# HGRN2 scores below level 16 on 32-key column tiles, and attention threads that begin 146 and 151 dense steps apart

## The chip, the core and the metric

The kernel runs on one core of a Trainium2 chip. The metric is device time in microseconds. The core has five engines with a queue each: TensorE (PE) for matmuls, VectorE (DVE), ScalarE (ACT), GpSimd (POOL) and SyncE (SP), which issues the DMAs here.

## What is computed

One layer of a hybrid decoder for a prompt of 256 tokens behind 16 meta tokens (one sequence) and for 8 single new tokens: SwiGLU half-step, mixer, SwiGLU half-step, each with a residual and a layer norm. The mixer projects 2048 features to ten blocks of 2048, runs 8 retention heads and 16 HGRN2 heads, gates both and projects back. The change lies in the HGRN2 heads, whose scores carry a decay for each pair of positions and feature:

```python
def hgrn2_chunk(S, q, k, v, logf):
    ...
    b = jnp.cumsum(logf.astype(jnp.float32), axis=2)
    causal = jnp.tril(jnp.ones((C, C), dtype=bool))
    diff = b[:, :, :, None, :] - b[:, :, None, :, :]
    decay = jnp.exp(jnp.where(causal[None, None, :, :, None], diff, -jnp.inf)).astype(q.dtype)
    A = jnp.einsum('bhid,bhjd,bhijd->bhij', q, k, decay)
    o = jnp.einsum('bhij,bhjv->bhiv', A, v) + jnp.einsum('bhid,bhdv->bhiv', q * jnp.exp(b).astype(q.dtype), S)
```

The new tokens take one step of the same recurrences on their own states (8 x 128 x 128 per HGRN2 head, 8 x 256 x 256 per retention head), which are read from and written back to memory.

## The kernel before

**Dense products.** All weights stream through one path: SP loads 512 KB (`raw`, L184, eight 128x128 blocks), ACT rounds it to a high part `whi` (L187), DVE takes the rest `wlo` (L188); each of these pools has three buffers. `dense` (L217) then issues three matmuls for a block, of 280 columns (16 meta, 256 prompt, 8 new tokens) or 264 where the meta tokens aren't needed. The columns are kept in two halves, one at an offset of `XH` = 148 elements (592 bytes) in tiles of `XP` = 296. The kernel is FFN 1 (0 to 758 us), mixer (758 to 1810), w_out and FFN 2 (1810 to 2607).

**The mixer** has eight units, each of one retention head and two HGRN2 heads. For unit u the program projects q, k, v, f (96 steps of dense, a step being one 128-feature slice for two outputs, six matmuls) and the gates of unit u-1 (64 steps). The attention work is written as two Python generators per unit, `mix_hg` and `mix_ret`. Each dense step calls `pump`, which counts down each running thread; a thread whose count is over issues its next piece of work, and the number that it yields is its next wait in steps. `start(generator, wait)` sets the first wait. So PE's order is fixed by these counts, and attention matmuls stand between dense ones. The order of the other engines' instructions is set by a scheduler from the program.

In unit 0, 32 steps are counted, in each later unit 160. HGRN2's thread starts when the value projection `i_h` is out, with a wait of 20 (unit 0), 46 (unit 1) or 3; retention's when `v_r` is out, with 24 (unit 1) or 3. That puts HGRN2's start at steps 20, 126, 243, 403 and on by 160, retention's at 35, 152, 291 and on by 160. A thread must be done before its gates' evacuation (L680 to L700) reads its output. Between pieces lie waits such as `W_LEVEL + 2 * (s <= 2 or u == 1) + calm`, with `calm` 2 in most units.

**Scores of HGRN2.** For level s, pairs of positions are those where the query lies in an odd block of s positions and the key in the even block ahead of it; K and Q are multiplied by products of f (the tiles T) as the level grows. Levels 16, 32 and 64 are matmuls on column tiles (L820, L825). Below that, before the change: the diagonal and levels 1 and 2 are five products q*k of 256 on DVE (`pr`, L239), split in high and low parts (ACT L224, DVE L225), and summed over the features on PE by a matrix of ones (L236, targets `pd` and `pl`); levels 4 and 8 are four fp32 matmuls of 128 keys by 192 columns (L801). Each result is masked into the score tile `acch` by DVE (L789, L883, L805). The high and low products live in the buffers `smh` and `vbh`, which also take the new tokens' states (`load`, L753 to L757).

**The new tokens' states.** DMAs bring the states (`smh`, `smr`), ACT scales them (L905, L1066), DVE adds k times v (L906, L1069), where v comes back from memory broadcast to all partitions (`vbh`, `vbr`); PE reads the result out in 32-column tiles (`pq` L932, `pqr` L1083).

Of the kernel before, what the change touches and what calls it, by code (L numbers as in the profile page):

```python
# [11 lines left out]
F32R = mybir.dt.float32r  # L12
# [6 lines left out]
P = 128  # L19
# [16 lines left out]
XP = 296  # L36
# [11 lines left out]
MASKS = {1: [0], 2: [1, MASKED], 4: [2], 8: [3, MASKED + 1]}  # L48
W_LEVEL = 6

# [77 lines left out]
def trunk(ctx: ExitStack, tc: tile.TileContext, A, O):  # L128
# [417 lines left out]
    with tc.tile_pool(name="yp", bufs=1) as yp:  # L546
# [7 lines left out]
        with tc.tile_pool(name="mp", bufs=1) as mp:  # L554
# [61 lines left out]
            def start(gen, wait):  # L616
                threads.append([gen, wait])

            def project(groups):
                for grp in groups:  # L620
# [4 lines left out]
                    if grp[0] == (QKV_ORDER[0], 0):  # L625
                        outs = norm1.first(block, outs, x0s)
                    elif grp[0] == (QKV_ORDER[2], 0):
                        v = st["i_h"] = tmp("v", (P, 2, T))
# [9 lines left out]
            def evacuate(n, c0, c1, o0, o1, b0, b1):  # L638
# [14 lines left out]
                elif n == "i_h":  # L653
                    v = st.pop("i_h", None)
                    if v is None:
                        v = tmp("v", (P, 2, T))
                        nc.scalar.copy(v[:, 0, :], o0)
                        nc.scalar.copy(v[:, 1, :], o1)

                    start(mix_hg(c0 // 2, st["f"], st["k"], st["q"], v), {0: 20, 2: 46}.get(c0, 3))  # L660
# [11 lines left out]
                elif n == "v_r":  # L672
                    v = tmp("v", (P, 2, T))
# [59 lines left out]
            def mix_hg(u, f, k, q, v):  # L733

                calm = 2 if u != 1 and u < HR - 1 else 0
# [49 lines left out]
                yield 9  # L785
                pd = mx_bank("pd")
                sums(pd, hilo, slice(0, 2))
                for h in range(2):
                    nc.vector.tensor_tensor(  # L789
                        out=acc[:, 2 * P * h : 2 * P * (h + 1)].rearrange("p (b c) -> p b c", b=2),  # L790
                        in0=pd.rearrange("p (b c h) -> p h b c", b=2, h=2)[:, h],
                        in1=ident.unsqueeze(1).to_broadcast([P, 2, P]), op=ALU.mult)
                Tt = f
                for s in LEVELS:
                    if s == 4:


                        for h in range(2):
                            pl = mx_bank("pl")
                            for b in range(2):  # L800
                                nc.tensor.matmul(  # L801
                                    pl[:, 192 * b : 192 * b + 192], K[:, h, NMETA + b * P : NMETA + b * P + P],
                                    Qm.rearrange("p i (x c) -> p i x c", x=4)[:, :, 2 * h + b, :], start=True, stop=True)
                            for i, (sl, mi) in enumerate(((4, MASKS[4][0]), (8, MASKS[8][0]), (8, MASKS[8][1]))):
                                nc.vector.copy_predicated(  # L805
                                    acc[:, 2 * P * h : 2 * P * (h + 1)].rearrange("p (b n t s) -> p b n t s", b=2, t=2, s=sl)[:, :, :, 1, :],
                                    msk[:, mi, :P].rearrange("p (b n s) -> p b n s", b=2, s=sl),
                                    pl[:, :384].rearrange("p (b i n s) -> p b i n s", b=2, i=3, s=sl)[:, :, i])
                    elif s != 8:
                        pl = mx_bank("pl")  # L810
# [4 lines left out]
                    for h in range(2 if s > 8 else 0):  # L815
# [12 lines left out]

                    if s == NMETA:
                        Tt = Tt[:, :, 1:]  # L830
                    k0 = 0 if s < NMETA else NMETA
                    n = LP - k0
                    nb = n // s
                    m = nb // 2
                    t2 = Tt[:, :, :nb].rearrange("p h (n t) -> p h n t", t=2)
                    kv = K[:, :, k0:].rearrange("p h (n t s) -> p h n t s", t=2, s=s)
                    qv = Q.rearrange("p h (n t s) -> p h n t s", t=2, s=s)
                    mq = SEQ // (2 * s)
                    mul(kv[:, :, :, 0, :], kv[:, :, :, 0, :], t2[:, :, :, 1].unsqueeze(3).to_broadcast([P, 2, m, s]))
                    if s != 4:  # L840
                        mul(qv[:, :, :, 1, :], qv[:, :, :, 1, :], t2[:, :, m - mq :, 0].unsqueeze(3).to_broadcast([P, 2, mq, s]))
                    Tn = tmp(f"T{2 * s}", (P, 2, m))
                    mul(Tn, t2[:, :, :, 0], t2[:, :, :, 1])
                    Tt = Tn
                    if s == 1:

                        q4 = Q.rearrange("p h (n t i) -> p h n t i", t=2, i=2)[:, :, :, 1, :]
                        hilo = [tmp("prod" + t, (P, 2, SEQ), dt=F32R, tag=t, bufs=2) for t in ("smh", "vbh")]
                        for j in range(2):
                            pr = tmp(f"pr{j}", (P, SEQ))  # L850
                            mul(pr.rearrange("p (h n i) -> p h n i", h=2, i=2), q4,
                                K[:, :, NMETA + j :: 4].unsqueeze(3).to_broadcast([P, 2, SEQ // 4, 2]))
                            split(hilo[0][:, j], hilo[1][:, j], pr)
                    if s == 2:

                        Qm = tmp("Qm", (P, 3, 2 * P), tag="smh", bufs=2)
                        qf = Q.rearrange("p h c -> p (h c)")
                        odd = [qf.rearrange("p (n t s) -> p n t s", t=2, s=sl)[:, :, 1, :] for sl in (4, 8)]
                        nc.scalar.copy(Qm[:, 0, :].rearrange("p (n s) -> p n s", s=4), odd[0])
                        t4 = Tt[:, :, NMETA // 4 :].rearrange("p h (n t) -> p h n t", t=2)[:, :, :, 0]  # L860
                        q4 = Q.rearrange("p h (n t s) -> p h n t s", t=2, s=4)[:, :, :, 1, :]
                        mul(q4, q4, t4.unsqueeze(3).to_broadcast([P, 2, 32, 4]))
                        nc.scalar.copy(Qm[:, 1, :].rearrange("p (n s) -> p n s", s=8), odd[1])
                        t4 = Tt[:, :, NMETA // 4 :].rearrange("p h (n t) -> p h n t", t=4)[:, :, :, 1]
                        mul(Qm[:, 2, :].rearrange("p (h n s) -> p h n s", h=2, s=8),
                            Q.rearrange("p h (n t s) -> p h n t s", t=2, s=8)[:, :, :, 1, :],
                            t4.unsqueeze(3).to_broadcast([P, 2, 16, 8]))
                    if s in (4, 8):
                        pass
                    elif s == 64:  # L870
# [4 lines left out]
                    elif s >= 16:  # L875
# [4 lines left out]
                    else:  # L880
                        x = pl.rearrange("p (c j) -> p j c", j=2) if s == 2 else pl.rearrange("p (j c) -> p j c", j=2)
                        for j, mi in enumerate(MASKS[s]):
                            nc.vector.copy_predicated(  # L883
                                acc.rearrange("p (n t s) -> p n t s", t=2, s=s)[:, :, 1, :],
                                msk[:, mi, :].rearrange("p (n s) -> p n s", s=s),
                                x[:, j].rearrange("p (n s) -> p n s", s=s))
                    if s in (16, 32):
                        load(s // 32)
                    if s != 4:
                        yield W_LEVEL + 2 * (s <= 2 or u == 1) + calm  # L890
# [358 lines left out]
```

## Times and profile before

| what | value |
|---|---|
| runs | 2610.65 us median of 3 (2608.11 to 2611.9) |
| profiled execution | 2608.88 us, its span 2607.1 us, granted PE clock 0.999 |
| FFN 1 / mixer / w_out and FFN 2 | 0 to 758 / 758 to 1810 / 1810 to 2607 us |
| a steady unit of the mixer | 130.6 us for 160 dense steps |
| DMA | 206 GB/s on the mean |

How to read it: in a row of waits or of the chain, the first number is the start and the second the duration, in us. In a row of windows come the stretch, its length, and the busy time of PE, PEld (weight load), DVE, ACT and POOL with the number of instructions, then the granted clock, the DMA share and GB/s. In a row of groups: line, engine, operation, output and inputs, shapes and count, then busy us and mean ns of one, then the idle time ahead of them and what ended it. A matmul's recorded duration is longer than the distance to the next, since matmuls are pipelined; what one costs is read from the start of one to the start of the next. An fp32 matmul appears in the trace as two records. Line numbers are those of the kernel before.

### The profile page before, as it was taken

The page shows a single profiled execution, that of the slowest core. Times are in us where ns is not written, and L with a number is a line of the kernel's source. Part 1 is how long each engine was busy: PE and PEld are TensorE (multiplying, and loading weights), DVE is VectorE, ACT ScalarE, POOL GpSimd, SP SyncE. Part 2 cuts the span into 40 slices and gives each one's busy share as a digit, 9 for nine tenths or more (in the row PEclk, how much of TensorE's full clock was granted, in tenths as well). Part 3 has the DMA queues.
Part 4 walks back from the last instruction along what each step waited for, and adds up shares of the span by engine and source line. Part 5 has one row for each costly group of instructions (what it writes and reads, how often), then busy time and mean ns, then how long its engine had stood idle before and what let it go on. Part 6 is the DMA issues. An engine that isn't in the chain of part 4 may idle for free.

```text
span 2607.1 us, 54875 instructions
## 1 busy us (share of the span) xinstructions
PE 2586.9 (99%) x22744; PEld 2554.0 (98%) x22744; DVE 1723.9 (66%) x2907; ACT 1385.2 (53%) x2184; POOL 12.9 (0%) x62
## 2 busy tenths in 40 slices
PE   9999999999999999999999999999999999999999
PEld 9999999999999889999999999999999999999998
DVE  6454444565579787777777777776995555556555
ACT  5444444444456666766666666675564444444444
POOL 0000000000000000000000000000000000000000
PEclk9999999999999999999999999999999999999999
DMA  7555555555556676767676767666556666666664
GB/s 244 183 185 186 186 183 184 185 185 184 183 198 222 219 260 205 262 202 260 206 260 201 262 202 259 207 228 194 193 188 200 195 195 196 196 196 193 199 196 147
DMA packets 154587, 536.17 MB, mean 206 GB/s; under 512 B 17696, under 2 KB 25696, under 8 KB 154336
## 3 DMA queue, kind: packets, MB, share of 16 engines
q1 hardware_dynamic: 154048, 532.37, 63.1%
q8 instruction: 178, 2.92, 0.5%
q14 instruction: 73, 0.60, 0.1%
q10 hardware_dynamic: 288, 0.29, 0.0%
HBM read 501.99 MB, written 30.61 MB: 204 GB/s over the span
## 4 chain that ended last, share of the span: by engine, by line
PE 92%; DVE 4%; DMA 2%; ACT 2%; issue 1%; SPq 0%; POOL 0%; DVEq 0%; POOLq 0%; ACTq 0%
PE up L217 36%; PE dn L217 18%; PE pj_q_r L217 3%; PE wo L217 3%; PE pj_v_r L217 3%; PE pj_i_h L217 3%; PE pj_f L217 3%; PE pj_k_r L217 3%; PE pj_g_r L217 3%; PE pj_q_h L217 3%; PE pj_a_r L217 3%; PE pj_g_h L217 3%; PE pj_a_h L217 3%; DVE wlo L188 1%; DMA out_srp<-sro 1%; PE pqr L1083 1%
## 5 line engine op out<-in xcount | busy, mean ns | idle before, releaser
L188 DVE TENSOR_TENSOR wlo<-raw,whi 128x1024 fp32r<-128x1024 f32 (+1 forms) x869 | 1061.6, 1222 | 735.1 <-ACT whi L187 732.8
L187 ACT CAST whi<-raw 128x1024 fp32r<-128x1024 f32 (+1 forms) x870 | 905.5, 1042 | 906.5 <-PE up L217 415.2
L217 PE MATMUL up<-xh,wlo 128*128 128x280 f32 (+1 forms) x2624 | 725.7, 280 | 0.3 <-DVE wlo L188 0.3
L217 PE MATMUL up<-xh,whi 128*128 128x280 f32 (+1 forms) x2624 | 726.0, 280 | 0.0
L217 PE MATMUL up<-xl,whi 128*128 128x280 f32 (+1 forms) x2624 | 725.4, 279 | 0.0
L217 PEld LDWEIGHTS up<-xh,wlo 128*128 128x128 f32 x2624 | 492.6, 189 | 0.7 <-DVE wlo L188 0.7
L217 PEld LDWEIGHTS up<-xh,whi 128*128 128x128 f32 x2624 | 493.1, 189 | 0.0
L217 PEld LDWEIGHTS up<-xl,whi 128*128 128x128 f32 x2624 | 492.7, 189 | 0.0
L217 PE MATMUL dn<-hh,whi 128*128 128x280 f32 (+1 forms) x1376 | 384.7, 280 | 0.0
L217 PE MATMUL dn<-hl,whi 128*128 128x280 f32 (+1 forms) x1376 | 384.3, 279 | 0.0
L217 PE MATMUL dn<-hh,wlo 128*128 128x280 f32 (+1 forms) x1376 | 384.3, 279 | 0.0
L217 PEld LDWEIGHTS dn<-hh,whi 128*128 128x128 f32 x1376 | 260.1, 189 | 0.1
L217 PEld LDWEIGHTS dn<-hl,whi 128*128 128x128 f32 x1376 | 260.1, 189 | 0.1
L217 PEld LDWEIGHTS dn<-hh,wlo 128*128 128x128 f32 x1376 | 260.1, 189 | 0.0
L217 PE MATMUL pj_g_r<-xh,whi 128*128 128x264 f32 x256 | 76.7, 299 | 0.0
L217 PE MATMUL pj_v_r<-xh,whi 128*128 128x280 f32 x256 | 74.2, 290 | 0.0
L217 PE MATMUL pj_g_h<-xh,whi 128*128 128x264 f32 x256 | 73.5, 287 | 0.0
L217 PE MATMUL pj_v_r<-xh,wlo 128*128 128x280 f32 x256 | 72.4, 283 | 0.3 <-DVE wlo L188 0.3
L217 PE MATMUL pj_k_r<-xh,whi 128*128 128x280 f32 x256 | 72.7, 284 | 0.0
L217 PE MATMUL pj_k_r<-xh,wlo 128*128 128x280 f32 x256 | 72.4, 283 | 0.0
L217 PE MATMUL pj_v_r<-xl,whi 128*128 128x280 f32 x256 | 72.3, 283 | 0.0
L217 PE MATMUL pj_k_r<-xl,whi 128*128 128x280 f32 x256 | 72.3, 283 | 0.0
(403 smaller groups left out, 5283.4 us busy)
## 6 DMA issues: line engine op xcount, KB each, us to landing
raw<-in_w_up SPq DMA_DIRECT2D x343, 512.0 KB, 4.2
raw<-in_w_in SPq DMA_DIRECT2D x320, 512.0 KB, 4.0
raw<-in_w_dn SPq DMA_DIRECT2D x172, 512.0 KB, 3.5
smr<-in_sr SPq DMA_DIRECT2D x32, 512.0 KB, 5.6
out_srs<-smr SPq DMA_DIRECT2D x32, 512.0 KB, 4.8
raw<-in_w_out SPq DMA_DIRECT2D x32, 512.0 KB, 3.6
smh<-in_sg SPq DMA_DIRECT2D x16, 512.0 KB, 4.4
vbr<-vrd SPq DMA_DIRECT2D x16, 512.0 KB, 4.4
```

What stands on the lines that cost most here:

```text
L187: nc.scalar.copy(hi[:, j:jn, :], raw[:, j:jn, :])
L188: nc.vector.tensor_tensor(out=lo[:, j0:j1, :], in0=raw[:, j0:j1, :], in1=hi[:, j0:j1, :].bitcast(F32), op=ALU.subtract)
L217: nc.tensor.matmul(o, w, t, start=start, stop=stop)
L1083: nc.tensor.matmul(pq[32 * j : 32 * j + 32, :256], qdr[:, c, 32 * b : 32 * b + 32], sms[2 * e + c][:, j, :], start=e + c == 0, stop=e + c ...
```

## The change

Four things change.

1. The diagonal and levels 1, 2, 4 and 8 become fp32 matmuls on column tiles of 32 keys: for each tile of 32 keys, 48 columns (three sets of 16 queries, gathered by ACT and DVE in `Qm`), and for the first group 32 columns more, the queries at the keys' own positions, of which the diagonal is taken. The products `pr`, their split and the sums are gone.
2. The threads' first waits are set by formulas, and the waits inside are the same in all units (`CALM` = 2). HGRN2's thread now starts at steps 20, 166, 312, 458, 604, 750, 896 and 1043, retention's at 35, 186, 337, 488, 639, 790, 941 and 1092.
3. The values' tile `v` has two buffers.
4. `XP` is 288, so the halves lie 576 bytes apart.

```diff
-XP = 296
+XP = 288
...
-MASKS = {1: [0], 2: [1, MASKED], 4: [2], 8: [3, MASKED + 1]}
+MASKS = {1: [0], 2: [MASKED, 1], 4: [2], 8: [3, MASKED + 1]}
+CALM = 2
...
-                    start(mix_hg(c0 // 2, st["f"], st["k"], st["q"], v), {0: 20, 2: 46}.get(c0, 3))
+                    start(mix_hg(c0 // 2, st["f"], st["k"], st["q"], v), max(3, 100 - 7 * c0) if c0 else 20)
...
-                    v = tmp("v", (P, 2, T))
+                    v = tmp("v", (P, 2, T), bufs=2)
...
-                    start(mix_ret(c0 // 2, st["q_r"], st["k_r"], v), 24 if c0 == 2 else 3)
+                    start(mix_ret(c0 // 2, st["q_r"], st["k_r"], v), max(3, 67 - 9 * c0 // 2) if c0 else 3)
...
-                hilo = [tmp("prod" + t, (P, 3, SEQ), dt=F32R, tag=t, bufs=2) for t in ("smh", "vbh")]
-                for i in range(3):
-                    pr = tmp(f"pr{i}", (P, SEQ))
-                    if i < 2:
-                        mul(pr, q[:, i, :SEQ], k[:, i, NMETA:LP])
-                    else:
-                        mul(pr.rearrange("p (h c) -> p h c", h=2), Q[:, :, 1::2], K[:, :, NMETA::2])
-                    split(hilo[0][:, i], hilo[1][:, i], pr)
+                def side_by_side(s):
+                    x = tmp("Qm", (P, 3, 2 * P), tag="smh", bufs=2)
+                    part = lambda i, s: x[:, i, :].rearrange("p (h n s) -> p h n s", h=2, s=s)
+                    nc.scalar.copy(part(0, s), odd(s))
+                    scale_q(s)
+                    nc.scalar.copy(part(1, 2 * s), odd(2 * s))
+                    k0 = NMETA // s
+                    t4 = Ts[s][:, :, k0 : k0 + SEQ // s].rearrange("p h (n t) -> p h n t", t=4)[:, :, :, 1]
+                    mul(part(2, 2 * s), odd(2 * s), t4.unsqueeze(3).to_broadcast([P, 2, SEQ // (4 * s), 2 * s]))
+                    return x
+                def blocks(x, s, own=None):
+                    x = x.rearrange("p i (x j c) -> p i x j c", x=4, j=4)
+                    for h in range(2):
+                        pl = mx_bank("pl")
+                        half = pl[:, : 2 * 80].rearrange("p (b c) -> p b c", b=2)
+                        for b in range(2):
+                            for j in range(0, P, 32):
+                                kk = K[:, h, NMETA + b * P + j : NMETA + b * P + j + 32]
+                                o = half[j : j + 32, b, :48].rearrange("p (i c) -> p i c", i=3)
+                                nc.tensor.matmul(o, kk, x[:, :, 2 * h + b, j // 32, :], start=True, stop=True, tile_position=(0, j))
+                                if own is not None:
+                                    nc.tensor.matmul(
+                                        half[j : j + 32, b, 48:], kk, own[:, h, b * P + j : b * P + j + 32],
+                                        start=True, stop=True, tile_position=(0, j))
...
-                yield 9
-                pd = mx_bank("pd")
-                sums(pd, hilo, slice(0, 2))
...
-                                nc.tensor.matmul(
-                                    pl[:, 192 * b : 192 * b + 192], K[:, h, NMETA + b * P : NMETA + b * P + P],
-                                    Qm.rearrange("p i (x c) -> p i x c", x=4)[:, :, 2 * h + b, :], start=True, stop=True)
...
-                    if s == 1:
-                        sums(pl[:, :SEQ], hilo, 2)
-                    elif s == 2:
-                        sums(pl, hilo)
...
+                yield 10 + CALM
+                blocks(Q1, 1, q)
+                scale_q(2)
+                join(2)
+                Q4 = side_by_side(4)
+                scale_k(1)
+                scale_k(2)
+                yield 2 * W_LEVEL - 1 + CALM
+                blocks(Q4, 4)
+                join(4)
...
```

`scale_k(s)`, `scale_q(s)` and `join(s)` are the multiplications of K, Q and T that stood in the loop over the levels before; `odd(s)` is the view of Q's odd blocks. `blocks` also masks its results: one multiplication by the unit matrix of 256 for the diagonal in each head (only with `own`), and three copy_predicated of 128 in each head.

**PE, unit 2, the first scores of HGRN2.** Names: `pd` and `pl` are the score banks, `pj_..` the projections' banks. Before, the four sums stand among the steps of the projection q_r:

```order
L217 MATMUL pj_q_r_12263<-xh_13_9280,wlo_12404 128x264
L236 MATMUL pd<-prodsmh,ones_r 128x512
L236 MATMUL pd<-prodvbh,ones_r 128x512
L236 MATMUL pl<-prodsmh,ones_r 128x256
L236 MATMUL pl<-prodvbh,ones_r 128x256
L217 MATMUL pj_q_r_12262<-xh_14_9284,whi_12403 128x264
```

and in the changed kernel (whose lines 218, 808 and 810 are dense and the two matmuls of `blocks`):

```order
L218 MATMUL pj_a_r_12995<-xh_5_9248,wlo_13028 128x264
L808 MATMUL pl<-Qm,K 32x48
L810 MATMUL pl<-q,K 32x32
L808 MATMUL pl<-Qm,K 32x48
L810 MATMUL pl<-q,K 32x32
L808 MATMUL pl<-Qm,K 32x48
L810 MATMUL pl<-q,K 32x32
```

The pair of rows comes 16 times in one piece, each pair on one column tile and the next pair on the next of four; and the place has moved from q_r of the unit's own projections to the gates of the unit before (`pj_a_r`).

**DVE, unit 3, the updates of both threads between two weight loads.** `wlo` is the low half of a load of weights, `acch` the score tile, `smh` and `ks` the HGRN2 states and retention's scaled keys. Before, one load apart from the next:

```order
L188 TENSOR_TENSOR wlo_14549<-raw_14547,whi_14548 128x8x128
L906 SCALAR_TENSOR_TENSOR smh<-vbh,fk,smh 128x128 x5
L188 TENSOR_TENSOR wlo_14584<-raw_14582,whi_14583 128x8x128
L239 TENSOR_TENSOR K<-K,T_14444 128x2x8x16
L239 TENSOR_TENSOR Q<-Q,T_14444 128x16x16
L906 SCALAR_TENSOR_TENSOR smh<-vbh,fk,smh 128x128 x8
L188 TENSOR_TENSOR wlo_14664<-raw_14662,whi_14663 128x8x128
```

and in the changed kernel:

```order
L189 TENSOR_TENSOR wlo_15175<-raw_15173,whi_15174 128x8x128
L1011 SCALAR_TENSOR_TENSOR ks_8640<-pt,dec,ks_8640 24x128
L255 TENSOR_TENSOR vs_8641<-vt_8636,vs_8641 24x128
L1011 SCALAR_TENSOR_TENSOR ks<-pt,dec,ks 128x128
L240 TENSOR_TENSOR dtab<-psc,dtab 128x400
L973 TENSOR_REDUCE cen<-vt_8636 24x1
L1011 SCALAR_TENSOR_TENSOR ks<-pt,dec,ks 128x128
L974 TENSOR_SCALAR cen<-cen 24x1
L907 SCALAR_TENSOR_TENSOR smh<-vbh,fk,smh 128x128
L240 TENSOR_TENSOR gt<-gs,pj_g_r_14863 128x264
```

The second half of the state update `smh` stood alone between its loads; now it stands with retention's keys, the score table `dtab` and the gates of the unit before.

More of the change, by code (lines that the diff above doesn't have):

```diff
@@ new lines, in blocks @@
+                def blocks(x, s, own=None):
[12 more added lines that the diff above has]
+                                        start=True, stop=True, tile_position=(0, j))
+                        a = acc[:, 2 * P * h : 2 * P * (h + 1)]
+                        if own is not None:
+                            nc.vector.tensor_tensor(
+                                out=a.rearrange("p (b j c) -> p b j c", b=2, j=4),
+                                in0=half[:, :, 48:].unsqueeze(2).to_broadcast([P, 2, 4, 32]),
+                                in1=ident.rearrange("p (j c) -> p j c", j=4).unsqueeze(1).to_broadcast([P, 2, 4, 32]), op=ALU.mult)
+                        for i, (sl, mi) in enumerate(((s, MASKS[s][0]), (2 * s, MASKS[2 * s][0]), (2 * s, MASKS[2 * s][1]))):
+                            n = 16 // sl
+                            nc.vector.copy_predicated(
+                                a.rearrange("p (b j n t s) -> p b j n t s", b=2, j=4, t=2, s=sl)[:, :, :, :, 1, :],
+                                msk[:, mi, :P].rearrange("p (b j n s) -> p b j n s", b=2, j=4, s=sl),
+                                half[:, :, 16 * i : 16 * i + 16].rearrange("p b (n s) -> p b n s", s=sl).unsqueeze(2).to_broadcast([P, 2, 4, n, sl]))
@@ L784, in mix_hg @@
                     yield 1
-                yield 9
-                pd = mx_bank("pd")
-                sums(pd, hilo, slice(0, 2))
[L788 to L793, printed above, removed]
@@ new lines, in mix_hg @@
+                yield 10 + CALM
[8 more added lines that the diff above has]
+                join(4)
+                for s in (4, 8):
+                    scale_k(s)
+                scale_q(8)
+                join(8)
+                yield W_LEVEL + 4 + CALM
+                for s in LEVELS[MASKED:]:
+                    pl = mx_bank("pl")
+                    for h in range(2):
@@ L837, in mix_hg @@
[L837 to L867, printed above, removed]
@@ L868, in mix_hg @@
-                    if s in (4, 8):
-                        pass
-                    elif s == 64:
+                    scale_k(s)
+                    scale_q(s)
+                    join(s)
+                    if s == 64:
                         for b in range(2):
@@ L879, in mix_hg @@
                                 pl[j * s : (j + 1) * s, : 4 * s].rearrange("p (x s) -> p x s", x=4))
[L880 to L886, printed above, removed]
                     if s in (16, 32):
                         load(s // 32)
-                    if s != 4:
-                        yield W_LEVEL + 2 * (s <= 2 or u == 1) + calm
+                    yield W_LEVEL + CALM
+                Tt = Ts[2 * LEVELS[-1]]
                 on = tmp("on_h", (P, 2, TL), bufs=2)
```

62 lines of the change are left out of this document (30 added, 32 removed), and 2 rows, old and new, of the table rows.

## Prediction

> **What bounds the kernel now.** I read the profile's first and fourth parts (busy shares, the chain that ended last), then the windows by stage, the waits of TensorE (PE), the chain again inside single units, and the PE timeline around the instructions that the change replaces.
>
> ```profile
> PE 2586.9 (99%) x22744; PEld 2554.0 (98%) x22744; DVE 1723.9 (66%) x2907; ACT 1385.2 (53%) x2184; POOL 12.9 (0%) x62
> PE 92%; DVE 4%; DMA 2%; ACT 2%; issue 1%; SPq 0%; POOL 0%; DVEq 0%; POOLq 0%; ACTq 0%
> core 0: 2607.1 us, clock 0.999
> 758.00:866.00 108.00, 100.44 (x874) 95.29 (x873) 100.45 (x223) 70.12 (x139) 1.73 (x3) 1.00 0.67 221
> 866.00:972.00 106.00, 102.54 (x937) 97.44 (x936) 84.31 (x183) 69.84 (x145) 1.21 (x3) 1.00 0.67 227
> 1238.60:1368.30 129.70, 129.70 (x1191) 126.94 (x1191) 100.84 (x205) 83.66 (x158) 1.22 (x3) 1.00 0.70 232
> 1498.80:1629.40 130.60, 130.60 (x1191) 127.02 (x1190) 100.95 (x205) 83.61 (x158) 1.22 (x3) 1.00 0.70 231
> 1629.40:1760.00 130.60, 129.21 (x1187) 126.35 (x1186) 103.18 (x213) 87.75 (x164) 2.32 (x14) 1.00 0.66 218
> ```
>
> PE makes up 92% of the chain at a granted clock of 0.999. In a steady unit of the mixer (the third and fourth windows) it is busy in every microsecond, with VectorE (DVE) at about 101 of 130: what PE no longer issues there comes off the end, and DVE work comes off for nothing. Only two units and the last one are otherwise: PE lacks 7.56 us in 758 to 866, 3.46 in 866 to 972 and 1.39 in the last, 12.4 together. A unit is 160 dense steps in 130.6 us, so a step is 0.82 us.
>
> **The change part by part: PE.** What goes is told by the chain inside unit 3, and by the timeline where a burst stands among dense matmuls (columns: start, duration, what).
>
> ```profile
> 1282.49 0.43 PE pd L236 x2
> 1282.92 0.24 PE pl L236 x2
> 1290.23 0.43 PE pl L236 x2
> 1297.81 1.30 PE pl L801 x8
> ...
> 1304.55 0.28 PE L217 MATMUL pj_v_r<-xh,wlo 128*128 128x280 f32 x1
> 1304.76 0.39 PE L825 MATMUL pl<-Q,K 128*16 128x16 f32 x32
> 1305.08 0.39 PE L217 MATMUL pj_v_r<-xh,whi 128*128 128x280 f32 x1
> 1305.30 0.28 PE L217 MATMUL pj_v_r<-xl,whi 128*128 128x280 f32 x1
> 1305.42 0.28 PE L217 MATMUL pj_v_r<-xh,wlo 128*128 128x280 f32 x1
> ...
> 1220.78 0.28 PE L217 MATMUL pj_a_r<-xh,wlo 128*128 128x264 f32 x1
> 1220.98 1.08 PE L932 MATMUL pq<-smh,qdh 128*32 128x128 f32 x32
> 1221.99 0.38 PE L217 MATMUL pj_g_r<-xh,whi 128*128 128x264 f32 x1
> 1222.21 0.28 PE L217 MATMUL pj_g_r<-xl,whi 128*128 128x264 f32 x1
> ...
> L825 PE MATMUL pl<-Q,K 128*16 128x16 f32 x256 | 3.1, 178 | 0.7 <-DVE K L239 0.7
> L932 PE MATMUL pq<-smh,qdh 128*32 128x128 f32 x256 | 8.6, 276 | 0.0
> ```
>
> Removed per unit: 0.43 + 0.24 + 0.43 + 1.30 = 2.40 us. The four L801 matmuls in the code are eight records, so an fp32 matmul is two records, and one of 192 columns takes 1.30 / 8 = 162 ns, 0.85 ns a column.
>
> Added per unit: 16 matmuls of 48 columns and 16 of 32 for level 1 and 2, and 16 of 48 for levels 4 and 8; that is 96 records on four column tiles, in two bursts. Two bursts of before have this form. A dense matmul with 280 columns follows the one ahead by 0.12 us (1305.30 to 1305.42), with 264 by 0.113. From 1304.55 to 1305.30 the burst of 16 columns cost 0.75 - 2 x 0.12 = 0.51 us. Its 32 records start over 0.39 - 0.18 = 0.21 us, so 6.8 ns apart, and the other 0.30 us go to entering and leaving the tiled form. The burst pq cost 1.43 - 2 x 0.113 = 1.20 us; its 32 records start over 1.08 - 0.28 = 0.80 us, 26 ns apart, so each of four tiles starts one every 104 ns: 0.81 ns a column, the speed of L801, with the four tiles at once. Entering and leaving is 1.20 - 8 x 0.108 = 0.33.
>
> So the second burst is 8 rounds of four tiles x 41 ns (48 columns x 0.85) + 0.32 = 0.65 us. The first is 8 x (41 + 27) + 0.32 = 0.87 us. Sum 1.52; with a little for the short records I take 1.55. **PE wins 0.85 us per unit, 6.8 us in eight.** That rests on four tiles running side by side although x and own, four records in all, follow each other on one tile before the next tile has its turn; pq has only the two records of one matmul there. The other end: no overlap in the first burst, 16 x (2 x 41 + 2 x 27) ns = 2.18 us + 0.32, and the unit is 2.50 + 0.65 - 2.40 = 0.75 us worse, 6.0 us in all. Where only the last record of a tile runs beside the next tile's first, it is 16 x (41 + 41 + 27) ns = 1.74 + 0.32, and the unit is 0.31 us worse, 2.5 in all. I take the gain, since pq shows queued records of one tile not holding up the others.
>
> The Trainium skill, page TensorEngine Tiling (Array Packing), section Instruction Overhead, states about 60 cycles for each matmul however few its columns. Taken as 25 ns of the one PE queue per record (an estimate from that page, a cycle put at the 0.42 ns of a dense column), 96 records and two switches would be 3.0 us for 2.40 removed, and PE 5 us slower in eight units; but the 16-column burst has its records 6.8 ns apart, so here the figure could hold at most on one tile (4 x 6.8 = 27 ns), which leaves the sum as it is. The same page's section Key Properties has a change of tiling mode drain the engine; the 0.30 to 0.33 us per burst agree.
>
> **DVE and ACT.**
>
> ```profile
> L239 DVE TENSOR_TENSOR pr<-Q,K 128x256 f32<-128x256 f32 x24 | 9.6, 421 | 0.2
> L225 DVE TENSOR_TENSOR prodvbh<-pr,prodsmh 128x256 fp32r<-128x256 f32 x40 | 15.7, 417 | 0.0
> L883 DVE COPY_PREDICATED acch<-msk,pl 128x256 f32<-128x256 uint8 x24 | 17.6, 733 | 3.6 <-PE pl L236 3.5
> L805 DVE COPY_PREDICATED acch<-msk,pl 128x128 f32<-128x128 uint8 x48 | 11.3, 290 | 0.0
> L224 ACT CAST prodsmh<-pr 128x256 fp32r<-128x256 f32 x40 | 15.3, 405 | 13.3 <-DVE pr L239 13.1
> ```
>
> Per unit DVE loses five products (2.1 us), five low halves (2.1) and three wide copy_predicated (2.2); it gains one more product of 256 (0.4) and six copy_predicated of 128 (1.7): 4.3 us less. ScalarE (ACT) loses five casts (2.0) and gains two copies of a like size (0.8). In steady units this is worth nothing by itself, since PE covers it. The tiles' new stride (576 B for 592) I cost at nothing: a dense matmul takes 0.12 / 280 = 0.43 ns a column at 592 B, the sums of 512 columns 0.215 / 512 = 0.42 at 1024 B, where the halves alternate. Only the 256-column sum shows more, 0.12 / 256 = 0.47; a tenth on every dense matmul would be over 200 us, and no stride seen does that. v in two buffers and the masks' order add no instruction.
>
> **The new starts.** In units 2 to 6 the HGRN2 thread began 51 dense steps into the unit, the retention thread 48 after it, and the pair repeated each 160. Now they repeat each 146 and 151; in unit 2 HGRN2 begins 120 steps in, retention 25 behind, so for units 1 to 4 both threads' DVE work falls on the same loads. In units 0 and 1 it is looser: 40 steps more between the first two HGRN2 threads.
>
> ```profile
> PE pqr L1083 <- DVE smr L1069: 3.0, 3, 1.9
> PE psr L1048 <- DVE ks L1012: 1.6, 2, 1.0
> PE pl L825 <- DVE Q L239: 1.6, 1, 1.6
> PE pt L1006 <- DVE acch L805: 1.5, 1, 1.5
> 923.43 5.46 DMA smh<-in_sg
> ...
> 932.04 1.23 DVE wlo L188
> ...
> 933.95 1.28 DVE acch L805 x6
> ...
> 960.61 6.28 DMA vbr<-vrd
> ...
> 967.46 1.03 PE pqr L1083 x4
> ```
>
> Two waits of unit 1 come straight from HGRN2 work that stood in DVE's queue (pl on Q 1.6, pt on acch 1.5); I take those 3.1 us as gone. Bounds: nothing, and all 12.4. On the other side stands the crowding: between the rows above, unit 1 has its loads of state, its copy_predicated, the low halves of the weights (wlo, on which dense matmuls wait) and the retention update together on DVE, and PE lost 3.46 us for it. Behind a waiting smr on DVE stands the next wlo, and PE waits for that once its three buffers are used. I take 0.4 us in each of units 1 to 5, 2 us, near the nothing of steady units because 30 us of DVE are free in each and its work falls by 4.3; the other end is 3.46 in each, 17.3.
>
> **Sum.** -6.8 - 3.1 + 2.0 = -7.9 us. The profiled execution took 2608.88 us (span 2607.1 and 1.8 around it): 2601.0. The median of the three runs, 2610.65, is 1.77 above it: **2602.8 us**.
>
> **Rivals.**
> - *Crowding decides (slower).* Place: units 1 to 5, where the smh and smr updates, ks and the level copies of both threads now stand between the same wlo. Price: unit 1's 3.46 each, 17.3, less the gain 6.8 and 3.1: +7.4, 2618 us. It decides from 9.9 us of new waits. For: in the changed order of unit 3 the smh and ks updates alternate, as the rows above show. Against: DVE has 30 us free per unit, and dense products keep three loads ahead.
> - *The tiles do not overlap.* +2.5 to +6.0 for PE instead of -6.8, with the waits as in the sum: 2612 to 2616 us. For: four records in a row on one tile, which no row shows. Against: pq. The Trainium skill's 60 cycles per matmul (TensorEngine Tiling (Array Packing), Instruction Overhead), if they fell one after another, would come out here too; I give that 0.02 of this rival's chance.
> - *All waits of units 0, 1 and 7 go.* -6.8 - 12.4: 2591 to 2596 us. Against: DVE is busy 100.45 of 108 us in the first window, with normalization and its first loads, which the change hardly touches.
> - *The change doesn't pay as it says:* the saved time is eaten by waits of equal size elsewhere, since PE then asks for weights sooner; 2608 to 2611. Against: steady units show no wait at all and DMA shares of 0.70.
>
> **How the numbers follow.** Forecast 0.50 (its own range 2599 to 2607, 0.42 of it below 2605.4), all waits gone 0.13, no overlap 0.12, crowding 0.17, nothing 0.08. A measurement of this kernel can tell about 0.2%, 5.2 us. Faster: 0.42 + 0.13 = 0.55. Slower, above 2615.9: all of crowding, and a third of no overlap for the waits that may come on top, 0.21. Same: the rest, 0.24. From 2593 to 2617 leaves out half of the waits-gone case and half of crowding, some 0.15.
>
> **What would show it.** In a steady unit: the level-1 burst as one piece of about 0.55 us and the level-4 one of 0.33, with dense matmuls back at 0.12 behind each, and the unit 0.85 us shorter wherever PE has no wait. If the first burst takes over 1.7 us, the tiles did not overlap. PE rows waiting for wlo, smr or smh in units 2 to 5 would show crowding; a first window with over 104 us of PE busy would show more waits gone. Dense matmuls off 0.12 us apart would prove me wrong on the stride.

## The result and the profile after

The changed kernel takes **2633.84 us** (median of 4 runs, 2632.35 to 2634.92) against 2609.38 us for the kernel before (2607.12 to 2611.9): a ratio of 1.0091, 95% interval 1.008 to 1.0103. It is 24 us slower, where 2602.8 was forecast. In the profiled execution the span went from 2607.1 to 2633.0 us. The page of the changed kernel, busy shares and chain:

```profile
PE 2594.6 (99%) x23400; PEld 2551.5 (97%) x23400; DVE 1703.5 (65%) x2859; ACT 1368.5 (52%) x2154; POOL 13.7 (1%) x62
PE 84%; DMA 6%; DVE 5%; ACT 3%; issue 2%; SPq 0%; POOL 0%; DVEq 0%; ACTq 0%; POOLq 0%
```

PE's share of the chain fell from 92 to 84%; DMA, DVE and ACT gained it. The waits of PE, by line and what it waited for:

```profile
PE pqr L1082 <- DVE smr L1068: 15.9, 12, 4.4
PE pl L872 <- DVE Q L240: 3.8, 1, 3.8
PE psr L1047 <- DVE ks L1011: 3.1, 4, 1.2
PE pl L808 <- DVE ks L1011: 1.4, 1, 1.4
PE ptk L900 <- DVE K L240: 1.3, 1, 1.3
```

Here psr is the product that gives retention's new prompt state, pqr the read-out of the new tokens' states, `ks` retention's scaled keys, and ptk a transpose of HGRN2's keys. Before, pqr waited 3.0 us in all, psr 1.6. These are the waits of PE's matmuls; pqr's loads of weights (PEld) waited longer, and already before. Their rows, before and changed:

```profile
PEld pqr L1083 <- DVE smr L1069: 12.6, 34, 2.4
PEld pqr L1082 <- DVE smr L1068: 31.1, 47, 4.8
```

Two units by window, where before PE was busy throughout (columns as in the prediction's windows):

```profile
1096.40:1232.70 136.30, 132.42 (x1289) 126.84 (x1288) 99.38 (x205) 80.76 (x158) 1.48 (x3) 0.99 0.69 227
1232.70:1375.60 142.90, 136.87 (x1288) 130.05 (x1288) 101.78 (x210) 87.29 (x165) 1.31 (x4) 0.96 0.68 223
```

A steady unit of 129.7 or 130.6 us is now one of 136 or 143. The same DVE work of about 100 us lies in it, and the granted clock is under 1.

A ledger shows where the time went: the distance from each matmul's start to the next one's, summed over the matmuls of one kind (worked out from the traces; us; the third column is the first experiment below).

| kind | before | changed | changed, old starts |
|---|---|---|---|
| scores below level 16 (sums and L801; L808 and L810) | 18.3 | 12.2 | 10.6 |
| pqr | 29.0 | 50.0 | 24.7 |
| psr | 13.4 | 17.3 | 12.7 |
| pvr, sums for retention's normalization | 3.1 | 1.8 | 1.8 |
| dense of the projections | 912.6 | 920.9 | 912.0 |
| FFN 1, up and gate | 958.2 | 959.1 | 960.7 |
| all, to the last matmul | 2600.6 | 2626.5 | 2588.0 |

The new scores are cheaper, 6.1 us with a wait of 1.4 in them; pqr gives back 20.9 and psr 3.9. PE's own waits for pqr grew by 12.9 us, those of its weight loads by 18.5. The bursts themselves, from the timeline of the changed kernel (first the pieces of the level-1 burst's beginning and end, then the level-4 burst):

```profile
1327.82 0.28 PE L218 MATMUL pj_a_r<-xh,wlo 128*128 128x264 f32 x1
1328.02 0.31 PE L808 MATMUL pl<-Qm,K 128*32 128x48 f32 x8
1328.13 0.25 PE L810 MATMUL pl<-q,K 128*32 128x32 f32 x7
...
1328.87 0.38 PE L218 MATMUL pj_g_r<-xh,whi 128*128 128x264 f32 x1
1329.09 0.28 PE L218 MATMUL pj_g_r<-xl,whi 128*128 128x264 f32 x1
...
1337.63 0.28 PE L218 MATMUL pj_a_h<-xh,wlo 128*128 128x264 f32 x1
1337.84 0.55 PE L808 MATMUL pl<-Qm,K 128*32 128x48 f32 x32
1338.32 0.38 PE L218 MATMUL pj_g_h<-xh,whi 128*128 128x264 f32 x1
1338.54 0.28 PE L218 MATMUL pj_g_h<-xl,whi 128*128 128x264 f32 x1
```

The first costs 1329.09 - 1327.82 - 2 x 0.113 = 1.04 us, the second 0.68: 1.72 for 1.55 forecast, and 2.40 removed. The four tiles do run side by side: the whole first burst took 1.04 us, and one record after another it would have been 2.50 by the prediction's own rates.

### The profile page after: what moved, and what is told of

Read it like the earlier page. It is cut to its first block, busy times and chain, and to the rows that moved or that the text cites. A ratio compares the mean times of both kernels' runs of the same rounds, so it can differ in the third digit from the quotient of the medians.

```text
span 2633.0 us, 56076 instructions
## 1 busy us (share of the span) xinstructions
PE 2594.6 (99%) x23400; PEld 2551.5 (97%) x23400; DVE 1703.5 (65%) x2859; ACT 1368.5 (52%) x2154; POOL 13.7 (1%) x62
## 4 chain that ended last, share of the span: by engine, by line
PE 84%; DMA 6%; DVE 5%; ACT 3%; issue 2%; SPq 0%; POOL 0%; DVEq 0%; ACTq 0%; POOLq 0%
PE up L218 34%; PE dn L218 18%; PE pj_i_h L218 3%; PE pj_q_r L218 3%; PE wo L218 3%; PE pj_k_r L218 3%; PE pj_v_r L218 3%; PE pj_q_h L218 3%; PE pj_g_r L218 2%; PE pj_a_r L218 2%; DVE wlo L189 2%; PE pj_g_h L218 2%; DMA vbr<-vrd 2%; PE pj_f L218 2%; PE pj_a_h L218 2%; DMA smh<-in_sg 2%
```

## The experiments

**Starts or scores.** First the two halves of the change apart. The changed kernel with the old starts:

```diff
-  start(mix_hg(...), max(3, 100 - 7 * c0) if c0 else 20)
+  start(mix_hg(...), {0: 20, 2: 46}.get(c0, 3))
-  start(mix_ret(...), max(3, 67 - 9 * c0 // 2) if c0 else 3)
+  start(mix_ret(...), 24 if c0 == 2 else 3)
```

> The changed kernel with the first waits of before (20, 46, 3 for HGRN2; 24 and 3 for retention); the new scores, the waits inside, the two buffers and the stride stay. Theory A (the new starts cost the time: retention's state update has to be done a fixed number of steps after its thread's start, and now its loads and its DVE work cross those of the HGRN2 thread): about 2604 us, 6 below before, since the new scores alone save 6.0 us of PE; PE's waits at the state read-out (pqr on smr) back at 3 to 5 us in all. Rival B (the rewritten scores, with their copies and masks, delay DVE and ACT whatever the starts): 2620 us or more, pqr waits still over 10.

Measured 2597.31 us, ratio 0.9955 (0.994 to 0.9969): faster than before, and 7 us below the 2604 of theory A; pqr's wait is 4.2, as theory A had it. And the other half, the kernel before with the new starts, the even waits, two buffers for v and `XP` = 288:

> The kernel before with the new first waits, the waits inside as changed, v in two buffers and the stride of 576 B (without which the buffers do not fit); the scores stay on DVE products and sums. Theory A: the starts bring about 30 us of waits, so 2636 to 2642 us, with pqr waits of 15 us or more. Rival B: within 5 us of before, 2606 to 2615.

Measured 2632.9 us, 1.009 (1.0075 to 1.0105); its pqr waits are 8.8 us, not the 15 expected, and its scores wait 6.6 us for Q. So the starts cost 23.4 us with the old scores (the even waits and the stride with them) and 36.5 with the new ones, and all else together wins 12. In the old-start kernel a steady unit has no wait of PE, and takes 128.3 to 129.3 us for 129.7 to 130.6 before:

```profile
1232.75:1362.00 129.25, 129.25 (x1274) 126.08 (x1272) 98.52 (x199) 82.20 (x154) 1.22 (x3) 1.00 0.70 234
1362.00:1490.25 128.25, 128.25 (x1274) 125.76 (x1272) 98.61 (x200) 82.38 (x154) 1.22 (x3) 1.00 0.71 236
```

**How retention's update comes late.** In each unit the state update is a chain: product psr, its copy to `sro` and store, the decay factor (which shares `sro`'s buffer), scaling on ACT, update of the first half on DVE, the second load of values (`vbr`, one buffer), update of the second half, then pqr. The program asks for pqr a fixed number of steps after psr, 23.8 us where nothing waits. In the steady units of before, the second half's updates begin 21 to 22 us after psr; in units 1 to 4 of the changed kernel 26 to 29. There was no room for that. PE's read-out in unit 3 before, and the same 29 records in the fastest kernel below:

```profile
1215.35 3.48 PE L1083 MATMUL pqr<-smr,qdr 128*32 128x256 f32 x29
1208.03 1.89 PE L1083 MATMUL pqr<-smr,qdr 128*32 128x256 f32 x29
```

Before, the last record starts 0.29 us behind the end of the last update in seven of eight units (0.34 in the eighth): the read-out already went at the pace of the updates, one each 0.40 us. A later read-out shows that the late update is all that pqr waits for:

```diff
-                yield 15 + 2 * CALM
+                yield 23 + 2 * CALM
```

> The changed kernel with one wait made longer: retention's state read-out comes 8 steps (6.6 us) later, nothing else. Theory A in its form that the chain of the state update (store of the new state, scale, load of the values, update, twice) is only too late for a fixed point in the program: the pqr waits of 15.9 us fall under 4 and the time to 2612 to 2618 us. Rival C (in the crowded stretch DVE or the DMA queues have too much work for the dense products as well): PE waits as long, then for wlo or further on, and the time stays above 2628.

Measured 2612.05 us, 1.0007 (0.9997 to 1.0016). The waits of pqr are gone; other waits (ptk 5.4, Q 3.7, psr 3.7, wlo 7.4) stay or grow. So the first part holds, with a part of the rival's.

**Which resource.** Three kernels took something from the crowded stretch of the changed kernel. First, less to store (a quarter of retention's and an eighth of HGRN2's new states):

```diff
-  nc.sync.dma_start(O["srs"][u, c, :, 4 * e : 4 * e + 4, :], sm)
+  nc.sync.dma_start(O["srs"][u, c, :, 4 * e : 4 * e + 1, :], sm[:, :1, :])
-  nc.sync.dma_start(O["sgs"][2 * u + h], sm)
+  nc.sync.dma_start(O["sgs"][2 * u + h, :, :1, :], sm[:, :1, :])
```

> The changed kernel with the new tokens' states written back only in part (a quarter of retention's, an eighth of HGRN2's), so that some 2.6 of about 8 MB of attention transfers per unit are gone. If the transfers crowd each other when both threads load and store at once: pqr waits under 6 us and the time at or under 2618 us. If the crowding is on DVE: 2626 to 2634.

Measured 2615.82 us, 1.0032 (1.002 to 1.0043); pqr no longer waits. Then seven of eight of HGRN2's updates on DVE left out (`if b == 0:` ahead of L907):

> The changed kernel without seven of eight of HGRN2's state updates on DVE (k times v isn't added there), some 14 instructions and 4 to 5 us of DVE per unit less, all in the stretch where the two threads cross; the transfers stay. If DVE's queue is what makes retention's update late: pqr waits under 6 us, at or under 2618 us. If it is the transfers: 2626 to 2634.

Measured 2635.77 us, 1.0108 (1.0093 to 1.0123), as slow as with them, and pqr still waits 12.2 us. **The amount of DVE work, on which I had put the crowding, isn't it**, as far as HGRN2's updates go. Then the factor in a tile of its own (`tmp("gam", (P, 1))` for `tmp("sro", (P, 1))`):

> The changed kernel with one tile more: the decay factor of retention's state update gets a buffer of its own, where it shared the one of the outgoing state and so was written only after that store had landed. If the chain of transfers in the retention thread (store, factor, scale, load of the values) is what comes too late at the read-out: pqr waits of 15.9 us fall to about 5 and the time from 2634 to 2612 - 2620 us. If the late part is DVE's queue or the second load of the values: 2628 to 2635.

Measured 2621.43 us, 1.0051 (1.0034 to 1.0068): pqr waits 3.3 us; 12 us are won where 14 to 22 were expected.

The store experiment changed something besides bytes: where the second load of values stands in SP's queue (it leaves 0.5 us after the start of the last update of the first half in all eight units). SP at the update of retention head 3, the changed kernel:

```profile
1237.21 0.64 SPq L1071 DMA_DIRECT2D out_srs<-smr  x1
1239.90 0.33 SPq L185 DMA_DIRECT2D raw<-in_w_in  x1
1240.28 0.43 SPq L1071 DMA_DIRECT2D out_srs<-smr  x1
1242.79 0.33 SPq L185 DMA_DIRECT2D raw<-in_w_in  x1
1243.17 0.45 SPq L1036 DMA_DIRECT2D vbr<-vrd  x1
```

and the same place before:

```profile
1203.93 0.34 SPq L1072 DMA_DIRECT2D out_srs<-smr  x1
1205.81 0.33 SPq L184 DMA_DIRECT2D raw<-in_w_in  x1
1206.61 0.34 SPq L1072 DMA_DIRECT2D out_srs<-smr  x1
1207.00 0.42 SPq L1037 DMA_DIRECT2D vbr<-vrd  x1
```

Before, vbr leaves 0.4 us behind the second store. In the changed kernel a weight load stands between them; it waits for its buffer until 1242.79, and vbr, whose own buffer is free from 1238.73, when the last update of the first half ends, waits behind it. From the start of that update to vbr's issue it is 0.9 to 1.2 us in units 1 to 6 of before (4.8 and 2.3 in units 0 and 7), and 6.5, 4.7, 4.8, 4.9, 4.6, 0.9, 0.9, 3.9 us in the changed kernel's eight units. DVE, the updates that follow in the changed kernel (start, duration, idle before):

```profile
1236.67 2.06 DVE L1068 SCALAR_TENSOR_TENSOR smr<-vbr,k_r,smr 128x256 f32<-128x256 f32 x5
1249.07 0.48 DVE L1068 SCALAR_TENSOR_TENSOR smr<-vbr,k_r,smr 128x256 f32<-128x256 f32 x1 [4.32 <-DMA vbr<-vrd]
```

Two kernels put that load elsewhere. On GpSimd's queue (`nc.gpsimd` for e = 1), and ahead of the weight load on SP:

```diff
-   nc.sync.dma_start(vbs[e], vrow[4 * e : 4 * e + 4, :].partition_broadcast(P))
+   with tc.high_priority():
+       nc.sync.dma_start(vbs[e], vrow[4 * e : 4 * e + 4, :].partition_broadcast(P))
```

> The changed kernel with one transfer on another queue: retention's second load of values (vbr, 512 KB) is issued by GpSimd, whose queue is nearly empty, and no longer by SyncE, where in units 0 to 4 and 7 it stood behind a weight load that waits for its buffer and left 3.9 to 6.5 us after it could have (0.9 us in units 5 and 6, and in the steady units of before). Theory Q (the place in SyncE's queue makes the state update late): the load leaves within 1 us, pqr waits fall from 15.9 to under 5 us, 2610 to 2620 us. Rival T (the transfers crowd each other, so the values land when they do whatever the queue): pqr waits over 10, 2627 us or more.

> The changed kernel with the same transfer kept on SyncE but given the weight loads' priority, so that it stands ahead of the weight load in units 0 to 4 and 7. Theory Q: as with GpSimd's queue, 2610 to 2622 us, unless the first load of values, which gets the priority too, holds weights back. Rival T: 2627 or more.

On GpSimd's queue: 2634.77 us, 1.0098 (1.0083 to 1.0113), nothing won: the time is rival T's, the shorter waits of pqr are theory Q's. First on SP: **2613.18 us**, 1.0016 (1.0007 to 1.0025), 20.7 us won, with vbr's issue 0.5 us behind the update's start in all units and pqr's waits at 0.3 us. The place in SP's queue is thus shown as the largest single cause (the edit gives the first load of values the same priority, but that one leaves 0.5 to 4.3 us ahead of psr here and 0.6 to 4.3 in the changed kernel). What is left, 15.9 us above the old starts, shows as waits for DVE: pl for Q 7.4 us, psr 4.2, ptk 3.9. No run tells what makes those late. GpSimd's load did leave early, 0.8 us behind the update's start, and pqr's waits fell to 4.5, but it took longer to land, 7.4 us at the median (5.5 to 9.1) against 4.2 (3.3 to 5.2) for SP's loads of values in the old-start kernel. DVE stood waiting for it longer, as its rows for the changed kernel and this one show, and PE's waits for wlo rose from 4.0 to 11.9 us:

```profile
DVE smr L1068 <- DMA vbr<-vrd: 19.8, 7, 4.3
DVE smr L1068 <- DMA vbr<-vrd: 31.3, 8, 6.3
```

In the old-start kernel the same move shows what then waits:

> The kernel of the old first waits with the new scores (2597.3 us) and the second load of values on GpSimd's queue. There only units 0 and 1 have it 6.5 and 4.9 us late, and only unit 0 waits (4.2 us): Theory Q 2592 to 2596 us, the steady units unchanged. Rival T: 2596 to 2600.

Measured 2614.27 us, 1.002 (1.001 to 1.0029): 17 us lost where 1 to 5 were to be won. DVE in unit 3, and PE's wait for it over the run:

```profile
1213.48 0.48 DVE L1068 SCALAR_TENSOR_TENSOR smr<-vbr,k_r,smr 128x256 f32<-128x256 f32 x1 [4.83 <-DMA vbr<-vrd]
1213.88 1.22 DVE L189 TENSOR_TENSOR wlo<-raw,whi 128x1024 fp32r<-128x1024 f32 x1
```

```profile
PE pj_g_r L218 <- DVE wlo L189: 12.5, 6, 2.7
```

The update waited 4.83 us for its values, and the weights' low half behind it in DVE's queue held up the dense product. The factor's own tile, which won 12 us in the changed kernel, loses time too with the old starts:

> The kernel of the old first waits with the new scores (2597.3 us) and the factor's own buffer. Its one wait at the read-out left is 4.2 us in unit 0, behind the same chain: if the chain's store is part of it, 2592 to 2596 us; if the second load of the values sets it alone, 2596 to 2599.

Measured 2613.03 us, 1.0019 (1.001 to 1.0028), 15.7 us lost. With the factor free early, ACT's scaling of the first half stands 75 to 108 us earlier and its first updates 1 to 4 us behind psr instead of 10 to 12, and PE now waits for wlo in the gates (4.1 us) and at the outputs (2.6). These waits are less than the loss; where the rest goes was not traced. And the two loosened together, in the changed kernel:

> The changed kernel with both links of retention's update loosened: the second load of values ahead of the weight load on SyncE (alone: 2634 to 2613 us), and the factor in a buffer of its own (alone: 2634 to 2621). If each removes waits of its own: 2598 to 2606 us. If both remove the same waits: 2610 to 2616 us, and what is left of the starts' cost lies elsewhere.

Measured 2620.11 us, 1.0049 (1.0032 to 1.0066): slower than the load's place alone, and above both ranges. They take away the same waits of pqr; that the factor's tile brings its own waits with it, as with the old starts, is my reading.

**Distance or spacing.** Retention 42 steps behind HGRN2 in unit 1 and 48 in the others, HGRN2 still every 146:

```diff
-  start(mix_ret(...), max(3, 67 - 9 * c0 // 2) if c0 else 3)
+  start(mix_ret(...), {2: 80}.get(c0, max(3, 100 - 7 * c0)) if c0 else 3)
```

> The changed kernel with retention starting 42 (unit 1) or 48 steps behind HGRN2 in every unit, as in before, while the HGRN2 threads keep their 146 steps. Theory A in its form that the small distance of 20 to 45 steps between the two threads makes them cross: pqr waits under 6 us, 2606 to 2613 us. Rival D (the spacing of 146 itself, by which the threads meet the evacuations of other projections, costs the time): 2625 us or more.

Measured 2618.64 us, 1.004 (1.0025 to 1.0055), between the two theories: 15 of the 36 us come back, pqr still waits 13.0. The opposite, threads every 160 steps and retention 20 behind HGRN2 (HGRN2's waits 52 in unit 1 and 31 from unit 2, retention's old ones):

> The new scores with threads that repeat every 160 steps as in before, but with HGRN2 starting so late in each unit that retention is only 20 steps behind it, as in the changed kernel's unit 1 (distance 15 in unit 0 as always). If the small distance makes the two threads stand in each other's way in the queues: 2612 to 2630 us, with the second load of values late by over 3 us in the steady units. If the spacing that is no multiple of a unit costs the time: 2597 to 2603 us.

Measured 2636.85 us, 1.0109 (1.0094 to 1.0124), slower than the changed kernel, 39.5 us above the old starts. So spacing that repeats with the unit doesn't help when the distance is small. The HGRN2 threads also stand 28 steps later in the unit here, which this run doesn't tell apart from the distance. The waits of PE in this kernel:

```profile
PE pl L808 <- DVE ks L1011: 10.6, 7, 2.0
PE pl L872 <- DVE Q L240: 10.3, 6, 2.2
PE pqr L1082 <- DVE smr L1068: 9.8, 4, 4.5
```

The first is a wait that no kernel with a distance of 48 has: HGRN2's scores `pl` take the bank in which retention's transposed keys lie until DVE's ks have read them (the rows name ks as the releaser; that it is the bank is my reading, since ks and pl share no other tile). vbr is 3.5 to 5.2 us behind the update in all later units here. So the small distance, or the later place that came with it, costs; the uneven spacing costs as well, by the 48-step kernel (21 us above the old starts). It was not tried which positions in a unit are bad, and why the old starts get their good place in SP's queue from unit 2 on stays open: a scheduler sets that order. Where threads repeat every 160 steps it comes out nearly the same in each unit, good (0.9 us with the old starts) or bad (3.5 to 3.6 here).

**A faster version.** The old starts with the read-out later, 8 steps in unit 0 and 2 in the others, and then with vbr ahead of the weight load too:

> The kernel of the old first waits with the new scores, with retention's read-out 8 steps later in unit 0 and 2 steps later in the others. If what is left there is only the read-out asked for too early, the 4.2 us of unit 0 and 0.3 to 0.9 us in each steady unit go: 2589 to 2594 us. If the wait only moves on to the next one that needs the same chain: 2595 to 2599.

> The fastest so far (old first waits, new scores, read-out 8 and 2 steps later: 2592.9 us) with the second load of values ahead of the weight load. Only units 0 and 1 have it late (6.5 and 4.9 us): 2588 to 2592 us. If giving it priority holds weights back: 2594 or more.

Measured 2592.94 us, 0.9936 (0.9921 to 0.9951), and **2590.38 us, 0.9928 (0.9913 to 0.9943)**, the lowest, though the two intervals overlap. In the latter pqr has no wait left, and its ledger row is 14.7 us for 29.0 before: of the 18 us won, 14 stand there, more than the scores gave. All units from the third on now take the same time:

```profile
1228.18:1356.43 128.25, 128.25 (x1274) 125.67 (x1272) 98.68 (x199) 82.62 (x155) 1.22 (x3) 1.00 0.70 235
1356.43:1484.68 128.25, 128.25 (x1273) 125.67 (x1272) 98.82 (x199) 82.76 (x154) 1.22 (x3) 1.00 0.70 236
```

## Why the prediction was wrong, point by point

- **PE's term was right.** -6.8 us forecast; the bursts of 1.72 us make it 0.68 per unit, 5.4 in eight, and the ledger has -6.1 with a wait in it. The rival that the tiles do not overlap is out (it wanted over 1.7 us in the first burst, which took 1.04), and with it the 3.0 us that the prediction worked out from the Trainium skill's overhead of each matmul, taken in series: 96 records took 1.72 us with both switches. The stride cost nothing: FFN 1's products, start to start, are 0.1161 us before and 0.1162 after.
- **The waits that would go:** 3.1 us were taken as gone, pl on Q 1.6 and pt on acch 1.5. In the changed kernel pl on Q is 3.8 and pt on acch 0.8. With the old starts, though, the new scores relieve more than I had put: that kernel is 12.2 us faster for 5.4 from the bursts, with pqr 4.4 less in the ledger, pvr 1.3 and psr 0.7.
- **The failed step is the new waits, "0.4 us in each of units 1 to 5, 2 us".** The starts cost 36.5. I argued that they were near the nothing of steady units since 30 us of DVE were free in each. That is a statement on the amount of work, and less of it did not help: with 14 DVE instructions fewer per unit nothing was won. What mattered most was the place of one load in SP's queue: put first, it gave back 20.7 us of the 36.5; 15.9 stay open.
- **"The nothing of steady units" was not nothing.** The prediction read PE's own waits and its busy share, and found none in steady units. Of the 12.6 us that pqr's weight loads waited for smr before, 4.8 stand in units 2 to 7. A busy share hides them, since a record of a matmul lasts longer than the distance to the next. The update had no slack there, so a delay that the new starts brought could go straight to PE.
- **The rival of crowding had the right sign and the wrong mechanism and size.** It priced each unit at unit 1's loss, 3.46 us, and put it on DVE. The runs show SP's queue first (20.7 us); for the rest the rows name DVE, and no run says why. The rows for it stood in the prediction itself: the chain in unit 1 runs through `vbr<-vrd`, 6.28 us, just ahead of pqr, and I read it as a crowded DVE. In units 2 to 7 before, the second half of the update began 1.4 to 2.7 us ahead of the read-out and ended 1.2 to 3.0 us after it began; a chain so close to its deadline turns a delay into a wait. SP's order, in which the load's place can be seen, does not occur in the prediction.
- The ends of the range came from unit 1's price; 2617 was too near by 17 us, since the price was that of another mechanism.

## What to carry to other kernels

Before moving a thread of work in time, take the chain that ends at its fixed read-out, count its slack in the trace, in the rows of the weight loads too (here it had none), and look in the new order at what stands ahead of each of its transfers in the issuing queue. A load whose buffer is free can stand behind one whose buffer isn't. Taking a wait out of one in-order queue may move it to another in which the critical work stands: only the run tells.

## What the runs showed of the hardware that I had not expected

After some waits PE came back at half speed. The changed kernel around the waits for pqr in unit 0, for Q in unit 2 and for pqr at the beginning of unit 4 (the last three columns are granted clock, DMA share, GB/s):

```profile
856.10:860.40 4.30, 0.00 (x0) 0.00 (x0) 1.14 (x3) 0.00 (x0) 0.00 (x0) 1.00 1.02 230
860.90:864.30 3.40, 3.40 (x16) 1.30 (x15) 2.94 (x8) 0.00 (x0) 0.00 (x0) 0.50 0.97 395
976.00:980.00 4.00, 0.21 (x12) 0.21 (x13) 3.39 (x7) 4.00 (x4) 0.00 (x0) 1.00 0.92 356
980.20:984.00 3.80, 3.80 (x24) 3.80 (x19) 3.17 (x10) 2.32 (x6) 0.00 (x0) 0.55 0.82 227
984.00:988.00 4.00, 4.00 (x41) 3.81 (x40) 1.36 (x2) 2.38 (x4) 0.00 (x0) 1.00 0.69 207
1247.00:1255.50 8.50, 5.17 (x28) 1.49 (x20) 5.96 (x12) 3.79 (x6) 0.00 (x0) 0.68 0.64 232
1255.80:1260.20 4.40, 4.40 (x20) 4.40 (x21) 1.98 (x11) 0.78 (x3) 0.00 (x0) 0.50 0.96 324
1260.30:1264.00 3.70, 3.70 (x33) 3.65 (x33) 1.39 (x2) 1.08 (x2) 0.00 (x0) 1.00 0.37 148
```

PE was idle or nearly so for some 4 us in the first two places, then had a granted clock of 0.50 or 0.55 for 3.4 to 3.8 us, then 1.00. In the third place the clock was already low in the stretch of waits, from 1250.0 on, behind a wait of 2.1 us. Dense matmuls start 0.22 us apart in the slow stretches instead of 0.113, 15 of them in the second place and 20 in the third, so that these two waits cost 1.6 and 2.1 us more in dense products than their own length: 3.7 of the 8.3 us that the dense row of the ledger gained. In the first place the low clock cost little: the read-out went at the pace of the updates on DVE, a matmul each 0.40 us, as at full clock in unit 3 before. With a fourth stretch (1120.3 to 1123.7, behind a wait of pqr of 2.4 us) the changed kernel has 20.5 us at half clock in the mixer, by its trace's record of the clock; the kernel before has none, the old-start kernel 6.8.

The Trainium skill, page TensorE: Matmul & The Clock Gate, section Part 1: The HAM clock gate, describes this: an idle window of about 3.4 us halves the clock, and one busy window restores it. The first two places agree with it, with waits of 4.4 and 3.8 us and 3.4 us at half clock behind each. The waits of 2.1 and 2.4 us were shorter than such a window and had half clock behind them too, while one of 2.5 us in the kernel with the later read-out (1083.0 to 1085.5) had not.

A load issued by GpSimd took 7.4 us to land at the median, SP's 4.2. The Trainium skill, page Trainium Kernel Development and Optimization, section Key Constraints, says that issuing from several engines saves only the sequencer's issue time, as all share the DMA engines; the load did leave earlier and took longer to land. The profile lists GpSimd's eight loads under a DMA queue of their own, of the kind software_dynamic, while SP's all go through one of the kind hardware_dynamic; no run here tells whether that is why they took longer.
